# Latent attention's keys, queries and values: per head in plain fp32, or per head pair from split operands through memory

## The chip, the cores and the metric

The program runs on one core of one Trainium2 chip. The metric is the device time of the whole program in microseconds (us), as the median of several runs. Engines are named as in the profile: PE (matmuls), PEld (its weight loads, which overlap PE), DVE, ACT, POOL, and SP, whose queue issues every DMA here.

## The reference

Two layers of a diffusion backbone over 1024 latent tokens and 256 context tokens (T = 1280), all in fp32. Each layer projects the modulated tokens, mixes them in three head groups, projects the result, and runs a gated convolution feed-forward. The change touches one of the three groups, latent attention, with 8 heads of 64 + 32 dimensions:

```
cq = _rms_norm(p[9], mla_q_norm_g)
q = _heads(jnp.einsum('blr,re->ble', cq, mla_w_uq), MLA_HEADS)
qn, qr = q[..., :MLA_D_NOPE], q[..., MLA_D_NOPE:]
ckv = _rms_norm(p[10], mla_kv_norm_g)
kn = _heads(jnp.einsum('blr,re->ble', ckv, mla_w_uk), MLA_HEADS)
v = _heads(jnp.einsum('blr,re->ble', ckv, mla_w_uv), MLA_HEADS)
...
s = (jnp.einsum('bqhd,bkhd->bhqk', qn, kn)
     + jnp.einsum('bqhr,bkr->bhqk', qr, kr)).astype(jnp.float32) * MLA_SCALE
p = jax.nn.softmax(s, axis=-1).astype(v.dtype)
return jnp.einsum('bhqk,bkhe->bqhe', p, v)
```

The rank of `cq` is 256 (two tiles of 128 rows) and that of `ckv` 128 (one tile). Layer 1 (the second) needs no context queries, so its queries begin at token 256.

## The kernel before

**Precision.** Most products are made from split operands: a tensor is held as `hi` (the value rounded to the type float32r, by an ACT cast) plus `lo` (the rest, by a DVE subtraction), which is `split`, L211 to L213. A product is then three float32r matmuls: hi times hi, hi times lo, lo times hi. The large projections (`dense`, L323) and the attention scores (L919) work so. A matmul of plain fp32 operands is one instruction in the program and two in the trace.

**Stages.** A layer goes through the input projection in two halves of 640 tokens (`proj`, a step for each 128 columns), linear attention and retention (`lin`), latent attention (`mla`), the output projection, and the feed-forward. `lin` and `mla` are Python generators: `mla` makes its first two steps at steps 11 and 12 of the second half's `proj` (`MLA_AT`), `lin` starts at step 13, and afterwards `weave` emits 1.1 steps of `lin` for each of `mla`. The Tile framework then schedules the emitted instructions: each engine's order is fixed when the program is built, and an engine runs its list in order. SP's queue is in order too: a DMA that waits for its data holds back all behind it.

**Latent attention.** `S.ckv` and `S.cq` are plain fp32 tiles in the pool `y` (8 buffers of 128 x 1280). For every pair of heads `prod_v` makes the values: 10 plain fp32 matmuls of 128 x 128 (L849) and two ACT copies (L852). For every four heads `prod_qr` makes the rotated part of the queries (L861, and L868 for the rotation). For every head `prod_kq` makes keys (64 rows, L894) and queries (64 rows, two terms, L897) and splits them out of PSUM by ACT (L903) and DVE (L904), each on 64 partitions. The product work of head h + 1 is the `side` generator of head h. Its rotated rows come by small DMAs from one SBUF tile to another (L883).

**A unit** is 128 queries of one head: scores (L919, three PSUM banks, the two halves of six banks in turn), maxima (DVE, L921 and L924), exponentials (ACT, L932), ten transposes (PE, L945), their copies (DVE L947, ACT L949), and the products with the values (L969). `lin_states` turns the linear group's keys in groups of two chunks: a DVE product, PE transposes (L600), an ACT copy (L602), PE products (L608), ACT copies (L615), all through one PSUM bank.

Pools that matter: `t` (6 buffers, shared by all passing results), `hid` (16), `y` (8), `h` (8: keys of two heads, queries of two heads), `wst` (4, raw weights; here 3 of them hold latent attention's weights to the end of the stage).

Of the kernel before, what the change touches and what calls it, by code (L numbers as in the profile page):

```python
# [19 lines left out]
T = 1280  # L20
# [54 lines left out]
class Net:  # L75
# [50 lines left out]
    def ws(self, shape):  # L126
        return self.sb.tile(shape, F32, tag="wst", bufs=4, name=self.nm("ws"))
# [37 lines left out]
    def wplan(self):  # L165
        """The split weights in the order of their use."""
# [81 lines left out]
    def ada(self, l, sets, alloc=None):  # L248
        """Modulation, for both kinds of tokens, of 1024 features at a time: of a section, or of a half of sections 0 and 1."""
# [39 lines left out]
    def modulate(self, l, sec, c0, c1, src, F):  # L289
        """F[k] = src(k) * (1 + scale) + shift; src(k) may be F[k] itself."""  # L290
# [25 lines left out]
    def dense(self, ps, segs, wu, h, ks=range(8)):  # L316
        """ps[:, i, :n] = w.T @ h[:, o:o + n] over 8 K tiles, or the ks of them, for the i-th (o, n) of segs."""
# [8 lines left out]
    def rstd(self, ps, segs, scale, eps, al):  # L326
        """(sum * scale + eps) ** -0.5 in SBUF."""
# [14 lines left out]
    def now(self, g):  # L342
        """The value of a generator that is emitted at once."""
# [14 lines left out]
    def begin(self, h, n):  # L358
        """The first half of K for the first n tiles of the projection: steps for their weights, then for a K tile of one."""
# [11 lines left out]
    def proj(self, l, b, h, S):  # L371
        """A step for every tile of the projection's columns."""
# [24 lines left out]
        def rms(tiles, segs, gcol, kn):  # L397
# [4 lines left out]
            for t in tiles:  # L402
                s = self.tt([128, W])
                nc.scalar.activation(s[:], t[:, c0 + o0:c0 + o0 + W], AF.Square)
# [4 lines left out]
            for i, t in enumerate(tiles):  # L409
                v = t[:, c0 + o0:c0 + o0 + W]  # L410
                nc.vector.scalar_tensor_tensor(v, v, self.vec[l][:, gcol + i:gcol + i + 1], r[:], op0=ALU.mult, op1=ALU.mult)

        def t3():
# [11 lines left out]
            # sums of log gates within chunks, [0] from the right and [1] from the left  # L425
# [59 lines left out]
        def copied(segs, dst):  # L485
            ps = mt(segs)
            for i, (o, n) in enumerate(segs):
                nc.scalar.copy(dst[:, c0 + o:c0 + o + n], ps[:, i, 0:n])

        late = []  # L490
        for m in PORDER:
# [12 lines left out]
            elif m == CKV:  # L504
                copied(full, S.ckv)
                g = None
            elif CQ <= m < CQ + 2:
                copied(qseg, S.cq[m - CQ])
# [23 lines left out]
            if m == CKV:  # L532
                late.append(lambda: rms([S.ckv], full, V_KVG, 1))
            if m == CQ + 1:
                late.append(lambda: rms(S.cq, qseg, V_QG, 2))
# [5 lines left out]
    def lin_tables(self, l, S):  # L541
# [10 lines left out]
        # rows of iota: t + 1, 127 - t, 128 - t, t;  lg: 0..1 by partition (fwd, bwd), 2 + 4 * dir + head  # L552
# [18 lines left out]
    def lin_states(self, l, S):  # L571
        """The chunks' k^T v sums, and from them the state before every chunk, in both directions."""
# [4 lines left out]
        for g in range(5):  # L577
# [4 lines left out]
            for r in range(2):  # L582
# [27 lines left out]
                # the sums lie where the state after their chunk belongs  # L610
# [18 lines left out]
    def lin_chunk_out(self, S, r, c, qv, cs, v, rhs, oS):  # L629
        """o (pair, chunk) = states' part + rhs(h)'s part, into oS."""  # L630
# [44 lines left out]
    def gla_out(self, l, S, g):  # L675
# [11 lines left out]
        def factors(ns):  # L687
            """[0]: q's factor exp(sum from the middle of its block of 2n), [1]: k times its factor."""
# [19 lines left out]
        def expands(i, ns):  # L708
            """q of every head in rows of its own, times its factor."""
# [46 lines left out]
        # products of neighbours and of equal tokens: their sums over a head are columns  # L756
# [69 lines left out]
    def mla(self, l, S):  # L826
        nc, a = self.nc, self.a
        ww = []
        for k, n in (("uqn", 512), ("uqr", 256), ("ukv", 512)):
            t = self.ws([128, 2, n])  # L830
            nc.sync.dma_start(t[:], a[k][l])
            ww.append(t)
        wn, wr, wk = ww
        Kt = [[self.hs([128, T]) for _ in range(2)] for _ in range(2)]
        lo = 0 if l == 0 else CTX
        V, Q, QR, ob = {}, {}, {}, {}
        flip = [0]

        def three(keep=False):
            b = flip[0] ^ 3  # L840
            if not keep:
                flip[0] = b
            return self.ps[:, b:b + 3, :].rearrange("p a b -> p (a b)")

        def prod_v(p):
            V[p] = [self.hid([128, 5, 128]) for _ in range(2)]
            ps = three(keep=True)
            for t_ in range(10):
                nc.tensor.matmul(ps[:, 128 * t_:128 * t_ + 128], S.ckv[:, 128 * t_:128 * t_ + 128], wk[:, 1, 128 * p:128 * p + 128],  # L849
                                 start=True, stop=True)  # L850
            for i in range(2):
                nc.scalar.copy(V[p][i][:].rearrange("p a b -> p (a b)"), ps[:, 640 * i:640 * i + 640])  # L852
            yield

        def prod_qr(x):
            QR[x] = [self.yk(F32R), self.yk(F32R)]
            ps, raw = three(keep=True), QR[x][1]
            chunks = [(o, min(512, T - o), ps[:, o - lo:min(512 + o, T) - lo]) for o in range(lo, T, 512)]
            for o, n, t in chunks:
                for kc in range(2):  # L860
                    nc.tensor.matmul(t, wr[:, kc, 128 * x:128 * x + 128], S.cq[kc][:, o:o + n], start=(kc == 0), stop=(kc == 1))  # L861
                nc.scalar.copy(raw[:, o:o + n].bitcast(F32), t)
            for o, n, t in chunks:
                r = raw[:, o:o + n].bitcast(F32)
# [7 lines left out]
                self.split(QR[x][0][:, o:o + n], raw[:, o:o + n], r)  # L872
                del t2, co, si
            yield

        def prod_kq(h):
            K = Kt[h % 2]
            Q[h] = [self.hs([128, T]) for _ in range(2)]
            rr = slice(32 * (h % 4), 32 * (h % 4) + 32)
            for x in range(2):  # L880
                for o in range(lo, T, 512):
                    c = slice(o, min(o + 512, T))
                    nc.sync.dma_start(Q[h][x][64:96, c].bitcast(F32), QR[h // 4][x][rr, c].bitcast(F32))  # L883
            if h < 2:
                for b in range(2):
                    cs = slice(640 * b, 640 * b + 640)
                    self.split(K[0][64:96, cs], K[1][64:96, cs], S.kr[b][64:96, :])
            if h == 1:
                S.kr.clear()
            yield  # L890
            ps = three(keep=True)
            for o, t, kb in ((CTX, ps[:, 0:512], 1), (CTX + 512, ps[:, 512:1024], 1), (0, ps[:, 1024:1280], 0)):
                n = 512 if kb else CTX
# [574 lines left out]
```

## Time and profile before

| | |
|---|---|
| time, median of 3 runs | 3469.18 us |
| lowest and highest run | 3468.41 and 3472.6 us |
| the profiled execution: first to last instruction | 3473.9 us |
| PE busy | 3383.5 us, 97% |
| DVE busy | 2227.2 us, 64% |
| ACT busy | 1548.3 us, 45% |
| DMA | 354.95 MB, mean 102 GB/s |
| stage of linear and latent attention, layer 0 | about 275 to 810 us |
| the same, layer 1 | about 2127 to 2608 us |

The profiled execution is a run of its own, and its span is the only time that is known of it. A row of the profile that merges instructions gives their start, the time from the first start to the last end, and their count. In a row of windows each engine has its busy time and its number of instructions.

### The profile page before, as it was taken

The numbers are of one execution on the slowest core, as the hardware profiler recorded it, in microseconds if no ns is written. First come the engines' busy times: TensorE is split into PE (matmuls) and PEld (weight loads), VectorE is DVE, ScalarE is ACT, GpSimd is POOL, SyncE is SP. The second block draws the span as 40 slices with busy tenths as digits, with TensorE's granted clock in tenths as the row PEclk, the third lists the DMA queues.
The fourth block names the chain that finished last, engine by engine and source line by source line (L and its number), as shares of the span: only waits on it lengthen the run. The fifth ranks groups of instructions, "written<-read, shape, count | busy, mean of one in ns | idle before, by whom it ended". The sixth has DMA issues, their size and how long they took to land. (4 is left out here: it accounts for less than half of the span.)

```text
span 3473.9 us, 58101 instructions
## 1 busy us (share of the span) xinstructions
PE 3383.5 (97%) x23454; PEld 2919.4 (84%) x23454; DVE 2227.2 (64%) x3787; ACT 1548.3 (45%) x2867; POOL 398.5 (11%) x627
## 2 busy tenths in 40 slices
PE   8999999989999999999999999999999999999998
PEld 6997666768999999899999898766777888888897
DVE  3435878776774444675557734788877765687555
ACT  3334555544453333343334444555563544345433
POOL 0000333331010000000000000333310000001001
PEclk9999999989999999999999999999999999999999
DMA  8654111124223333432223444111124333323331
GB/s 291 203 185 135 29 55 41 40 83 141 74 73 116 122 116 132 147 104 78 75 73 120 161 135 136 36 42 51 38 96 131 96 92 97 97 91 116 98 92 49
DMA packets 174990, 354.95 MB, mean 102 GB/s; under 512 B 15552, under 2 KB 92160, under 8 KB 174720
## 3 DMA queue, kind: packets, MB, share of 16 engines
q1 hardware_dynamic: 174720, 351.23, 31.7%
q8 instruction: 184, 3.01, 0.4%
q14 instruction: 86, 0.70, 0.1%
HBM read 310.01 MB, written 36.44 MB: 100 GB/s over the span
## 5 line engine op out<-in xcount | busy, mean ns | idle before, releaser
L323 PE MATMUL ps<-h,w 128*128 128x320 f32 (+5 forms) x9600 | 1667.4, 334 | 15.1 <-ACT h L212 6.3
L323 PEld LDWEIGHTS ps<-h,w 128*128 128x128 f32 x9600 | 1532.0, 190 | 145.7 <-issue 7.0
L213 DVE TENSOR_TENSOR w<-ws,w 128x1024 fp32r<-128x1024 f32 x360 | 440.1, 1223 | 590.5 <-PE ps L323 294.5
L1180 PE MATMUL ps<-hid,w 128*128 128x256 f32 (+4 forms) x3696 | 576.6, 316 | 1.5 <-ACT hid L212 1.5
L1180 PEld LDWEIGHTS ps<-hid,w 128*128 128x128 f32 x3696 | 538.9, 189 | 36.1 <-issue 7.6
L212 ACT CAST w<-ws 128x1024 fp32r<-128x1024 f32 x360 | 378.8, 1053 | 416.6 <-PE ps L1180 291.2
L919 PE MATMUL ps<-h,h 96*128 96x512 f32 (+1 forms) x1200 | 325.4, 392 | 18.7 <-DVE w L947 14.4
L919 PEld LDWEIGHTS ps<-h,h 96*128 96x128 f32 x1200 | 200.0, 194 | 78.1 <-issue 21.1
L1147 DVE SCALAR_TENSOR_TENSOR t<-u,vec,t 128x642 f32<-128x642 f32 (+3 forms) x176 | 144.6, 821 | 181.9 <-ACT t L1146 181.8
L932 ACT ACTIVATE w<-ps,sm 128x768 f32<-128x768 f32 (+2 forms) x272 | 208.9, 774 | 113.0 <-DVE sm L928 91.2
L1141 ACT COPY u<-ps 128x512 f32<-128x512 f32 (+4 forms) x264 | 118.2, 483 | 310.7 <-PE ps L323 310.7
L1185 DVE SCALAR_TENSOR_TENSOR y<-ps,mod,y 128x320 f32<-128x320 f32 (+5 forms) x376 | 197.0, 557 | 69.0 <-PE ps L1180 68.3
L945 PE MATMUL ps<-ident,w 128*128 128x128 f32 x1312 | 222.3, 287 | 12.1 <-ACT w L932 12.0
L945 PEld LDWEIGHTS ps<-ident,w 128*128 128x128 f32 x1312 | 152.0, 144 | 70.6 <-issue 35.5
L965 POOL TENSOR_SCALAR dg<-ident,sm 128x128 f32<-128x128 f32 x144 | 99.8, 697 | 954.7 <-DVE sm L963 833.4
L1137 POOL MEMSET u<- 128x1 f32 (+1 forms) x264 | 20.9, 102 | 1616.9 <-DVE t L1148 1462.4
L969 PE MATMUL ps<-w,hid 128*64 128x128 f32 x2624 | 196.8, 282 | 3.8 <-DVE y L979 2.0
L969 PEld LDWEIGHTS ps<-w,hid 128*64 128x64 f32 x2624 | 151.8, 139 | 41.2 <-issue 29.1
L921 DVE TENSOR_REDUCE sm<-ps 128x1 f32<-128x1024 f32 x128 | 156.3, 1221 | 43.8 <-PE ps L919 38.8
L949 ACT COPY w<-ps 128x256 f32<-128x256 f32 (+1 forms) x272 | 128.2, 474 | 94.0 <-PE ps L945 92.0
L716 POOL TENSOR_TENSOR hid<-hid,hid 128x512 f32<-128x512 f32 x108 | 146.3, 1371 | 98.5 <-ACT hid L696 69.0
L1146 ACT ACTIVATE t<-u,vec 128x642 f32<-128x642 f32 (+3 forms) x176 | 153.8, 874 | 0.4
(195 smaller groups left out, 3279.4 us busy)
## 6 DMA issues: line engine op xcount, KB each, us to landing
ws<-in_up_dram SPq DMA_DIRECT2D x176, 512.0 KB, 3.6
ws<-in_down_dram SPq DMA_DIRECT2D x88, 512.0 KB, 3.5
ws<-in_ada_dram SPq DMA_DIRECT2D x80, 512.0 KB, 4.8
ws<-in_w_in_dram SPq DMA_DIRECT2D x48, 512.0 KB, 4.3
ws<-in_w_out_dram SPq DMA_DIRECT2D x32, 512.0 KB, 3.7
y<-in_ada_dram SPq DMA_DIRECT2D x16, 512.0 KB, 8.3
ws<-in_w_v_dram SPq DMA_DIRECT2D x16, 512.0 KB, 4.0
hid<-in_xT_dram SPq DMA_DIRECT2D x16, 320.0 KB, 6.1
```

The lines of the kernel that those rows point to most:

```text
L212: self.nc.scalar.copy(hi, src)
L213: self.nc.vector.tensor_tensor(lo, src, hi.bitcast(F32), op=ALU.subtract)
L323: nc.tensor.matmul(ps[:, i, 0:n], w_[:, k, :], h[k][:, part, o:o + n], start=(k == 0 and q == 0), stop=(k == 7 and q == 2))
L716: nc.gpsimd.tensor_tensor(X[n][:], blk(E[n][:, 0, cs[i]]), qx[:], op=ALU.mult)
L919: nc.tensor.matmul(sc[:, o:o + n], q[qa][0:96, qs], K[ka][0:96, o:o + n], start=(x == 0), stop=(x == 2))
L921: nc.vector.tensor_reduce(st[:, 1:2], sc[:, 0:1024], axis=AX.X, op=ALU.max)
L932: nc.scalar.activation(P[:, c0:c1], sc[:, c0:c1], AF.Exp, bias=st[:, 2:3], scale=MSCALE, accum_out=st[:, 3 + j:4 + j])
L945: nc.tensor.transpose(ps[:, t_], P[:, 128 * (t0 + t_):128 * (t0 + t_) + 128], self.ident[:])
L969: nc.tensor.matmul(op[64 * i:64 * i + 64, 0], V[h // 2][t_ // 5][:, t_ % 5, r:r + 64], pts[i][:, t_], start=(t_ == 0), stop=(t_ == nk - 1) ...
L1146: nc.scalar.activation(v[:, 0:n], u[:, 1:1 + n], AF.Identity, scale=cw(j, 1), bias=self.vec[l][:, V_CB + j:V_CB + j + 1])
L1180: nc.tensor.matmul(pb[i][:, 0:n], w[w_][:, x, ms], p.hh[f0 + x][hp][:, o - 1:o - 1 + n], start=(x == 0 and q == 0), stop=(x == gn - 1 and ...
L1185: nc.vector.scalar_tensor_tensor(t, pb[i][:, o:o + n], self.md(l, 5, m, who), t, op0=ALU.mult, op1=ALU.add)
```

## The change

Latent attention's low-rank inputs and its weights are now held split, and its products are made as three float32r matmuls for a pair of heads (128 rows at once) or, for the values, for all heads (512 columns at once). The results go out of PSUM as split pairs into `t` tiles and by DMA into DRAM tiles (`S.kq`, `S.qr`, `S.vm`); each head's keys and queries, and each pair's values, come back by DMA.

- `copied` puts the projected columns into `hid` tiles; `rms` normalises there and splits into `S.ckv` (2 tiles of `y`) and `S.cq` (4 tiles of `y`).
- `first()` makes all keys, all values, the rotated queries of heads 0 to 3 and the queries of pair 0, and loads head 0. `rest()`, the side work of head 0, makes all other queries. Heads 1 to 7 have loads alone as side work (`following`).
- The products use one bank at a time of the three that are free (`bank`).

The core of the diff (lines in which only a comment goes are left out):

```diff
+        def rms(tiles, segs, gcol, kn, dst):
...
+                v, c = t[:, o0:o0 + W], slice(c0 + o0, c0 + o0 + W)
                 nc.vector.scalar_tensor_tensor(v, v, self.vec[l][:, gcol + i:gcol + i + 1], r[:], op0=ALU.mult, op1=ALU.mult)
+                self.split(dst[i][0][:, c], dst[i][1][:, c], v)
...
+        def prod_v():
+
+            t = [self.hid([128, 512], F32R) for _ in range(2)]
+            weight("v", a["ukv"][l][:, 1], [[x[:]] for x in t], 1)
+            for t_ in range(10):
+                p = bank()
+                for x, (wa, ca) in enumerate(order):
+                    nc.tensor.matmul(p, S.ckv[ca][:, 128 * t_:128 * t_ + 128], W["v"][wa][0], start=(x == 0), stop=(x == 2))
+                s = self.tt([128, 512])
+                nc.scalar.copy(s[:], p)
+                nc.sync.dma_start(S.vm[:, t_, :], s[:])
...
+        def product(p, o, n, terms):
+            for x, (w_, c) in enumerate(terms):
+                nc.tensor.matmul(p, w_, c[:, o:o + n], start=(x == 0), stop=(x == len(terms) - 1))
...
+        def to_memory(p, y, o0, terms):
+
+            for o in range(o0, T, 512):
+                n = min(512, T - o)
+                t = bank()[:, 0:n]
+                product(t, o, n, terms)
+                hi, lw = self.tt([128, 512], F32R), self.tt([128, 512], F32R)
+                self.split(hi[:, 0:n], lw[:, 0:n], t)
+                for x, s in enumerate((hi, lw)):
+                    nc.sync.dma_start(S.kq[:, p, y, x, o:o + n], s[:, 0:n].bitcast(F32))
...
-        def prod_kq(h):
-            K = Kt[h % 2]
...
-                nc.tensor.matmul(t[0:64, 0:n], wk[:, 0, 64 * h:64 * h + 64], S.ckv[:, o:o + n], start=True, stop=True, skip_group_check=True)
-                if o >= lo:
-                    for kc in range(2):
-                        nc.tensor.matmul(t[64:128, 0:n], wn[:, kc, 64 * h:64 * h + 64], S.cq[kc][:, o:o + n],
...
+            for x in range(2):
+                nc.sync.dma_start(Kt[h % 2][x][0:64].bitcast(F32), S.kq[rows, h // 2, 0, x])
+                nc.sync.dma_start(Q[h][x][0:64, lo:T].bitcast(F32), S.kq[rows, h // 2, 1, x, lo:T])
+                nc.sync.dma_start(Q[h][x][64:96, lo:T].bitcast(F32), S.qr[rot, h // 4, x, lo:T])
...
+        def first():
+            weights()
+            prod_k(0)
+            yield
+            prod_qr(0)
+            prod_q(0)
+            load(0)
+            yield
+            prod_v()
+            yield
+            for p in (1, 2, 3):
+                prod_k(p)
+            load_v(0)
+            S.ckv.clear()
+            yield
```

How the instructions stand now. PE at the entry of layer 0's latent attention, before: a group of `lin_states` (L600 its transposes, L608 its products, `hid` its keys) has scores (L919) and transposes (L945) between its parts.

```order
L600 MATMUL ps<-ident,hid_2980 128x128 x4
L919 MATMUL ps<-h_2549,h_3032 128x256
L945 MATMUL ps<-ident,w_3094 128x128 x2
L608 MATMUL ps<-hid_2978,hid_2986 32x64 x16
L945 MATMUL ps<-ident,w_3112 128x128 x2
L969 MATMUL ps<-w_3096,hid_2552 64x128
L919 MATMUL ps<-h_2548,h_3032 128x512
```

PE at the same place now (L992 is the scores' new line, L604 and L612 are L600 and L608, L872 is the values' product): five groups follow the first scores, and the values' 30 matmuls follow them.

```order
L992 MATMUL ps<-h_2567,h_2774 128x256
L604 MATMUL ps<-ident,hid_2948 128x128 x4
L612 MATMUL ps<-hid_2946,hid_2956 32x64 x16
L604 MATMUL ps<-ident,hid_3034 128x128 x4
L612 MATMUL ps<-hid_3032,hid_3040 32x64 x16
L604 MATMUL ps<-ident,hid_3068 128x128 x4
L612 MATMUL ps<-hid_3066,hid_3076 32x64 x16
L604 MATMUL ps<-ident,hid_3102 128x128 x4
L612 MATMUL ps<-hid_3100,hid_3108 32x64 x16
L604 MATMUL ps<-ident,hid_3137 128x128 x4
L612 MATMUL ps<-hid_3135,hid_3152 32x64 x12
L872 MATMUL ps<-hid_3154,y_374 128x512
```

No other work of PE stands between the parts of those five groups any more; behind L872's 30 matmuls come the 27 of the keys of pairs 1 to 3. SP's queue at that entry, before: loads for `lin_states` (L584, L586, L580) between the small moves into a head's query tile (L883).

```order
L580 DMA u_2939<-gB_91 128x2x256
L883 DMA h_3032<-y_2620 32x256
L883 DMA h_3033<-y_2621 32x512 x2
L584 DMA hid_2908<-rqk_90 128x256
L586 DMA hid_2910<-v_88 128x2x256
L883 DMA h_3033<-y_2621 32x256
L883 DMA h_3212<-y_2620 32x512 x2
```

SP's queue now, at the end of the keys' products of pairs 1 to 3 (L930 stores a split part of them, L881 loads the values of pair 0, L588 and L590 are L584 and L586).

```order
L930 DMA kq_372<-t_3297 128x512
L930 DMA kq_372<-t_3298 128x512
L930 DMA kq_372<-t_3306 128x512
L930 DMA kq_372<-t_3307 128x512
L930 DMA kq_372<-t_3315 128x256
L930 DMA kq_372<-t_3316 128x256
L881 DMA hid_3321<-vm_373 128x5x128
L881 DMA hid_3322<-vm_373 128x5x128
L588 DMA hid_3325<-rqk_90 128x256
L590 DMA hid_3327<-v_88 128x2x256
```

The load of the first values has moved behind all 10 stores of values and all 18 stores of these keys.

## Rows read from the trace of the kernel before

**Rows 1.** The page's first part: busy time of each engine.

```profile
PE 3383.5 (97%) x23454; PEld 2919.4 (84%) x23454; DVE 2227.2 (64%) x3787; ACT 1548.3 (45%) x2867; POOL 398.5 (11%) x627
```

**Rows 2.** Windows: both attention stages; then clock granted, DMA share, GB/s.

```profile
285.00:345.00 60.00, 55.30 (x542) 38.55 (x541) 39.48 (x82) 32.10 (x93) 3.80 (x5) 0.97 0.48 148
345.00:810.00 465.00, 439.72 (x3683) 320.27 (x3682) 363.15 (x792) 248.86 (x637) 166.37 (x174) 0.97 0.17 52
2140.00:2200.00 60.00, 55.32 (x573) 41.22 (x571) 39.16 (x85) 30.70 (x92) 3.29 (x5) 0.86 0.40 121
2200.00:2550.00 350.00, 337.91 (x2870) 244.71 (x2870) 285.25 (x580) 190.97 (x467) 127.90 (x130) 1.00 0.15 44
2550.00:2608.00 58.00, 57.23 (x539) 46.79 (x538) 44.39 (x102) 39.09 (x93) 8.82 (x12) 1.00 0.32 110
```

**Rows 3.** Product matmuls by line: counts, nanoseconds min/median/max, first and last start, forms.

```profile
L849 PE MATMUL ps<-ws,y x160: 272/275/377, 275.0 to 2493.2; 128*128 128x128 f32 x160
L861 PE MATMUL ps<-y,ws x40: 379/592/697, 282.9 to 2362.9; 128*128 128x512 f32 x32, 128*128 128x256 f32 x8
L894 PE MATMUL ps<-y,ws x96: 378/592/644, 308.6 to 2541.8; 128*64 128x512 f32 x64, 128*64 128x256 f32 x32
L897 PE MATMUL ps<-y,ws x160: 379/592/645, 312.9 to 2542.8; 128*64 128x512 f32 x128, 128*64 128x256 f32 x32
```

**Rows 4.** Chain that ended last: plain fp32 products in unbroken runs (512 columns at L861).

```profile
2126.60 2.23 PE ps L849 x20
...
2134.50 3.43 PE ps L861 x8
```

**Rows 5.** Timeline of PE: float32r matmuls of 256 and of 512 columns, unbroken.

```profile
261.78 13.36 PE L454 MATMUL ps<-w,h 128*128 128x256 f32 x112
...
2845.89 44.48 PE L323 MATMUL ps<-h,w 128*128 128x512 f32 x192
```

**Rows 6.** By line: ACT and DVE work on products, and casts and subtractions of 512.

```profile
L852 ACT COPY hid<-ps x16: 669/698/712, 277.0 to 2493.9; 128x640 f32<-128x640 f32 x16
L862 ACT COPY y<-ps x10: 372/585/586, 284.9 to 2363.6; 128x512 f32<-128x512 f32 x8, 128x256 f32<-128x256 f32 x2
L903 ACT CAST h<-ps x56: 348/1005/1013, 316.6 to 2545.8; 64x1024 fp32r<-64x1024 f32 x32, 64x256 fp32r<-64x256 f32 x24
L904 DVE TENSOR_TENSOR h<-ps,h x56: 402/1216/1226, 317.6 to 2547.7; 64x1024 fp32r<-64x1024 f32 x32, 64x256 fp32r<-64x256 f32 x24
L212 ACT CAST y<-y x10: 406/619/622, 292.2 to 2370.9; 128x512 fp32r<-128x512 f32 x8, 128x256 fp32r<-128x256 f32 x2
L213 DVE TENSOR_TENSOR y<-y,y x10: 424/692/694, 292.8 to 2372.1; 128x512 fp32r<-128x512 f32 x8, 128x256 fp32r<-128x256 f32 x2
```

**Rows 7.** Timeline: one group of lin_states.

```profile
301.45 0.60 PE L600 MATMUL ps<-ident,hid 128*128 128x128 f32 x4
...
302.14 0.59 ACT L602 COPY hid<-ps 128x512 f32<-128x512 f32 x1 [1.87 <-PE ps L600]
...
302.78 0.65 PE L608 MATMUL ps<-hid,hid 128*32 128x64 f32 x32
...
303.50 0.56 ACT L615 COPY y<-ps 128x64 f32<-128x64 f32 x4 [0.24 <-PE ps L608]
```

**Rows 8.** DMA issues: count, size each, median us from issue to landing.

```profile
hid<-v SPq DMA_DIRECT2D x20, 256.0 KB, 4.1
...
m<-hid SPq DMA_DIRECT2D x18, 256.0 KB, 2.1
h<-y SPq DMA_DIRECT2D x64, 64.0 KB, 2.0
```

**Rows 9.** Windows: layer 1's entry, and the stretch with the busiest DMA.

```profile
2160.00:2170.00 10.00, 7.83 (x92) 4.01 (x91) 7.63 (x13) 6.11 (x17) 0.00 (x0) 0.99 0.62 202
2170.00:2180.00 10.00, 8.91 (x56) 6.52 (x54) 6.53 (x13) 2.31 (x8) 0.00 (x0) 0.50 0.39 115
2180.00:2190.00 10.00, 9.58 (x101) 7.89 (x102) 5.89 (x16) 7.00 (x22) 1.26 (x2) 0.66 0.21 66
1960.00:1980.00 20.00, 18.25 (x107) 17.36 (x105) 17.66 (x29) 9.74 (x15) 2.09 (x2) 0.96 0.96 346
```

More of the change, by code (lines that the diff above doesn't have):

```diff
@@ L532, in proj @@
             if m == CKV:
[L533 removed]
+                late.append(lambda: rms(ckv, full, V_KVG, 1, [S.ckv]))
             if m == CQ + 1:
[L535 removed]
+                late.append(lambda: rms(cq, qseg, V_QG, 2, S.cq))
             yield
@@ L845, in prod_v, with weight @@
-        def prod_v(p):
+        lo = 0 if l == 0 else CTX
+        order = ((0, 0), (0, 1), (1, 0))
+        W = {}
+        def weight(key, src, t, parts):
+            for p in range(parts):
+                raw = self.tt([128, 512])
+                nc.sync.dma_start(raw[:], src[:, p] if parts > 1 else src)
+                self.split(t[0][p], t[1][p], raw[:])
+            W[key] = t
+        Kt = [[self.hs([128, T]) for _ in range(2)] for _ in range(2)]
+        V, Q, ob = {}, {}, {}
+        flip, ring = [0], [0]
@@ new lines, in three, with weights @@
+        def three():
+            flip[0] ^= 3
+            return self.ps[:, flip[0]:flip[0] + 3, :].rearrange("p a b -> p (a b)")
+        def weights():
+            t = [self.hid([128, 512], F32R) for _ in range(2)]
+            weight("r", a["uqr"][l].rearrange("p k n -> p (k n)"), [[x[:]] for x in t], 1)
+            t = self.ws([128, 2, 512], F32R)
+            weight("k", a["ukv"][l][:, 0], [[t[:, 0]], [t[:, 1]]], 1)
+            t = [self.ws([128, 2, 512], F32R) for _ in range(2)]
+            weight("n", a["uqn"][l], [[x[:, 0], x[:, 1]] for x in t], 2)
@@ new lines, in bank @@
+        def bank():
+            ring[0] = (ring[0] + 1) % 3
+            return self.ps[:, (flip[0] ^ 3) + ring[0], :]
+        def prod_v():
+            t = [self.hid([128, 512], F32R) for _ in range(2)]
+            weight("v", a["ukv"][l][:, 1], [[x[:]] for x in t], 1)
[6 more added lines that the diff above has]
+                nc.sync.dma_start(S.vm[:, t_, :], s[:])
+            W.pop("v")
@@ L846, in prod_v, with load_v @@
+        def load_v(p):
             V[p] = [self.hid([128, 5, 128]) for _ in range(2)]
[L847 to L850, printed above, removed]
             for i in range(2):
-                nc.scalar.copy(V[p][i][:].rearrange("p a b -> p (a b)"), ps[:, 640 * i:640 * i + 640])
-            yield
+                nc.sync.dma_start(V[p][i][:], S.vm[:, 5 * i:5 * i + 5, 128 * p:128 * p + 128])
@@ L863, in prod_qr @@
-            for o, n, t in chunks:
-                r = raw[:, o:o + n].bitcast(F32)
+            terms = [(W["r"][wa][0][:, 256 * kc + 128 * x:256 * kc + 128 * x + 128], S.cq[kc][ca]) for kc in range(2) for wa, ca in order]
+            for o in range(lo, T, 512):
+                n = min(512, T - o)
+                t = bank()[:, 0:n]
+                product(t, o, n, terms)
+                raw = self.hid([128, 512], F32R)
+                r = raw[:, 0:n].bitcast(F32)
+                nc.scalar.copy(r, t)
@@ L905, in prod_kq, with rest, following @@
+        def rest():
+            load(1)
+            S.kr.clear()
+            prod_q(1)
+            yield
+            prod_q(2)
+            yield
+            prod_qr(1)
+            yield
+            prod_q(3)
+            S.cq.clear()
+            yield
+        def following(h):
+            load(h)
+            if h % 2 == 0:
+                load_v(h // 2)
             yield
@@ L917, in scores @@
                 n = min(512, nk - o)
-                for x, (qa, ka) in enumerate(order):
+                for x, (ka, qa) in enumerate(order):
                     nc.tensor.matmul(sc[:, o:o + n], q[qa][0:96, qs], K[ka][0:96, o:o + n], start=(x == 0), stop=(x == 2))
@@ L983, in values @@
                 nc.sync.dma_start(S.m[:, 4 + h // 2, c0:c1], o[:, c0:c1])
-        def chain(*gs):
-            for g in gs:
-                yield from g
-        for _ in chain(prod_v(0), prod_qr(0), prod_kq(0)):
+        for _ in first():
             yield
@@ L1285 @@
         nc.sync.dma_start(S.gw[64:96], a["gw"][l])
-        S.cq = [net.yk(), net.yk()]
-        S.ckv = net.yk()
+        S.qr = net.dp.tile([128, 2, 2, T], F32, name=f"qr{l}")
+        S.kq = net.dp.tile([128, 4, 2, 2, T], F32, name=f"kq{l}")
+        S.vm = net.dp.tile([128, 10, 512], F32, name=f"vm{l}")
+        S.ckv = [net.yk(F32R) for _ in range(2)]
+        S.cq = [[net.yk(F32R) for _ in range(2)] for _ in range(2)]
         F = []
```

89 lines of the change are left out of this document (30 added, 59 removed).

## The prediction, on record before the run

> **What bounds the kernel now.** I read the page's first part for the whole span, then windows over the two stages that the change touches, then the chain of waits. PE is busy for 97% of the span and no other engine for more than 64% [rows 1]. In the windows of linear and latent attention the reader is to see the same: of 993 us PE is busy for 945, DVE for 771, and even the last stretch, where latent attention runs alone, is PE's (57.2 of 58.0 us) [rows 2]. So a microsecond taken from PE there is worth nearly one, unless its list then waits. The slack is unequal, though: DVE is at 78 and 82% in the long stretches of both layers, and PE already stands idle for 25 of 465 and 12 of 350 us there [rows 2].
>
> **What is removed from PE.** The products' records by line are 160, 40, 96 and 160 [rows 3]; a plain fp32 matmul is two records. One record costs 2.23 / 20 = 0.112 us at 128 columns and 3.43 / 8 = 0.429 at 512 [rows 4]; at 256 I take half, 0.214. Values (L849): 160 x 0.112 = 17.8 us. Rotated queries (L861): 32 x 0.429 + 8 x 0.214 = 15.4. Keys (L894): 64 x 0.429 + 32 x 0.214 = 34.3. Queries (L897): 128 x 0.429 + 32 x 0.214 = 61.8. Together 129.3 us over both layers. The rotation (L868) stays as it is.
>
> **What is added to PE.** Three terms per product, but for two heads at once. Keys are 24 matmuls of 512 and 12 of 256 columns a layer, queries 48 and 24 in layer 0 and 48 and none in layer 1, rotated queries 24 and 12, then 24 and none, values 30 of 512 a layer: 252 of 512 and 60 of 256 columns. A float32r matmul costs 44.48 / 192 = 0.232 us at 512 and 13.36 / 112 = 0.119 at 256 [rows 5]: 58.4 + 7.2 = 65.6 us. **PE saves 129.3 - 65.6 = 64 us**, about 34 in layer 0 and 30 in layer 1.
>
> **ACT and DVE.** Casts and subtractions now work on 128 partitions. DVE loses L904, 32 x 1.22 + 24 x 0.40 = 48.7 us, and gets 32 x 0.69 + 12 x 0.42 = 27.2 for keys and queries, 10 x 0.69 for the split weights and, scaled from 512 to 640 columns, at most 12 x 0.87 for the splits in `rms` [rows 6]: 5 us less. ACT loses L903, 40.5, and L852, 11.2; it gets 24.7 + 6.2 + 9 in the same way and 20 x 0.585 for the values' copies [rows 6]: about nothing. The splits in `rms` lie beside the projection's matmuls; if that cover were gone, they would cost 12 x 0.77 = 9 us. Neither engine pays for PE's saving, and neither gains as much as PE does.
>
> **What is added as waits: the entry of the stage.** All 64 us come out of heads 0 to 7, but the new waits stand in one place, between the last projections and the first full units of head 0, once per layer.
>
> (a) Five groups of `lin_states` now stand on PE with nothing between their parts. A group takes from 301.45 to 303.50 + 0.56 = 304.06, 2.61 us, of which PE works 1.25 [rows 7]; they share one PSUM bank, so the next cannot start sooner. 5 x 1.36 = 6.8 us a layer, 13.6 in all. Before, scores stood between. Bounds: 0, if their loads and steps are ready early and the bank's reader is quicker, and 20, if SP's queue, in which these loads stand behind head 0's, brings them later.
>
> (b) Keys of pairs 1 to 3: nine parts in a row, each needing two of the six `t` buffers until its two stores have landed. A buffer is held for a cast 0.62, a subtraction 0.69 and a landing of 2.1 us for 256 KB, with queueing some 4 us [rows 6, 8]; three parts are in flight, so nine take 12 us against 6 x 3 x 0.232 + 3 x 3 x 0.119 = 5.2 of matmuls. 6.8 a layer, 13.6 in all. Bounds: 0 and 30 (DMA below). The values' ten parts need one buffer each, and ACT's 10 x 0.585 is below PE's 30 x 0.232 = 7.0 [rows 5, 6]: 0.
>
> (c) The first scores wait for head 0's stores and loads, and the first products with values for the load of the values behind the keys' 18 stores. A store of 256 KB lands in 2.1 us and a load in 4.1 [rows 8]: 6.2. Head 0's is covered in the main by two parts of pair 1's queries and projections (I take 2 us open in layer 0, 1 in layer 1), the values' by about 4 us of scores and queries (1.5 open in each): 6 us. Bounds: 0 and 25.
>
> [...]
>
> (d) PE's clock. After a stretch with PE at 7.8 of 10 us, the granted clock was 0.50 and then 0.66 for 10 us each [rows 9], so the level of 1.2 GHz instead of 2.4 for about 17 us, which costs some 8 us of matmuls. Layer 1's entry pays this already, layer 0's mostly not (0.97) [rows 2]. I take 6 us more for layer 0. Bounds: 0 and 20.
>
> **Sum.** (a) to (d) are 13.6 + 13.6 + 6 + 6 = 39 us. The heads' later boundaries lose their product bursts and get a higher share of DVE; I let these cancel. 64 - 39 = 25 us. The profiled execution of 3473.9 us would become 3449; the median before is 4.7 us below that span, so the median after is 3444 us.
>
> **Rivals.**
>
> The entry is hidden. If the loads come early and the `t` buffers turn round in 2 us, the waits are 15 us or less, and the time falls by 49 us or more: 3405 to 3420. For it: DMA moves only 52 GB/s in the long stretch, and the entry had 121 to 148 [rows 2]. Against it: the order of PE's list, in which nothing can fill the gaps.
>
> DMA saturates at the entry, and the kernel is slower. Keys, values, the first queries and rotated queries, and two heads' loads are 5.2 + 2.6 + 2.6 + 1.3 + 3.2 = 15 MB a layer on top of the 148 GB/s that flow there [rows 2]. The fastest row of 20 us moved 346 GB/s at a share of 0.96 [rows 9]: 15 MB at the 200 GB/s left over take 75 us, of which PE's own work at the entry covers some 55 at best. If they are exposed for more than 64 / 2 = 32 us a layer, the change loses; at 40 a layer the time is 3469 + 16 = 3485. For it: (a), (b) and (c) all stand behind the same queue. Against it: most of those bytes are needed only by later heads, and only the `t` buffers make PE wait for their stores.
>
> DVE takes over. In the long stretches DVE would be busy for some 360 of 431 us (84%) in layer 0 and 282 of 320 (88%) in layer 1 [rows 2]. Where its in-order list sets the pace, a stretch shortens only by what DVE itself loses there, 48.7 - 27.2 - 6.9 = 15 us in place of 64. If that holds for half of them, the gain is (64 + 15) / 2 = 40, and the entry's 39 takes it all: 3468, and between 3462 and 3476 with its bounds. For it: PE's idle time in the long stretches. Against it: the scores need no more of DVE than before, and its list loses its pieces of 1.22 us, behind which maxima waited.
>
> **How the numbers follow.** The forecast, waits of 20 to 55 us, has 0.55: 3425 to 3462. The hidden entry has 0.20, DVE's case and others that end near zero 0.13, saturation 0.12. The range from 3412 to 3470 leaves out part of the hidden case's best (0.10) and most of the slower one (0.10). Runs of this kernel lie within 4 us, so 0.2%, 7 us, is about what can be told from no change: faster is 0.55 + 0.20 + a little of DVE's case = 0.77, slower 0.12 less what ends near zero, 0.10, same 0.13.
>
> **What would show it.** The new product lines should have about 310 records of 0.23 and 0.12 us, and PE's busy time in both stages should fall by 60 to 65 us. PE's idle time between the last projection and the first full units should rise by 10 to 20 us a layer, under `lin_states`' transposes and the keys' products, with waits on ACT, DVE and `t` stores. From head 1 on, PE's idle time should be as before. I would be wrong if the keys' parts come at PE's own pace (then the gain is larger), or if the long stretches lose PE's saving to waits on DVE (then smaller).

## The result, and the profile after

The changed kernel takes 3497.4 us (median of 4 runs, 3494.2 to 3503.4), the kernel before 3468.8 (4 runs, 3466.0 to 3472.6): a ratio of 1.0084, 95% interval 1.0070 to 1.0099. It is 29 us slower; 25 us faster had been forecast. The profiled execution has a span of 3492.3 us, 18.4 more than the one of before. The account below goes by these two profiles and so explains 18.4 of the 29 us: the one of before is a little slower than its 4 timed runs, the one of the changed kernel is the fastest of its 4.

The page of the changed kernel, first part [rows 1]:

```profile
PE 3363.4 (96%) x23310; PEld 2932.7 (84%) x23310; DVE 2225.3 (64%) x3797; ACT 1549.2 (44%) x2881; POOL 399.4 (11%) x627
```

PE's busy time fell by 3383.5 - 3363.4 = 20.1 us only. Its idle time, span less busy, rose from 90.4 to 128.9, by 38.5. Both together are the 18.4 us. So the waits came out near the 33 us that (a), (b) and (c) made, while of the saving of 64 us less than a third is left.

Windows of the changed kernel over the attention stages, in the columns of [rows 2]. The later starts and ends allow for what it is late:

```profile
285.00:345.00 60.00, 41.88 (x371) 34.12 (x370) 27.66 (x50) 22.31 (x67) 0.00 (x0) 0.75 0.84 240
345.00:822.00 477.00, 444.52 (x3783) 334.24 (x3784) 364.51 (x814) 255.63 (x669) 171.44 (x179) 0.95 0.34 101
2152.00:2212.00 60.00, 40.55 (x371) 31.16 (x369) 24.68 (x47) 27.44 (x76) 0.00 (x0) 0.72 0.80 235
2212.00:2567.00 355.00, 335.41 (x2948) 253.48 (x2948) 291.60 (x613) 190.18 (x489) 129.47 (x134) 0.98 0.34 98
2567.00:2625.00 58.00, 57.23 (x542) 46.83 (x540) 43.58 (x101) 39.90 (x94) 8.84 (x12) 1.00 0.27 91
```

In the entries PE stands idle for 18.1 and 19.5 of 60 us, where it was 4.7 and 4.7; its clock is 0.75 and 0.72, where it was 0.97 and 0.86; the DMA share is about twice what it was. The long stretches have some 15 us more idle time than before. Where it lies shows when the stages are cut at each layer's first exponential. Up to there, of the kernel before and then of the changed one:

```profile
275.00:325.00 50.00, 46.66 (x403) 36.28 (x401) 27.23 (x51) 23.45 (x65) 0.00 (x0) 0.97 0.53 164
2127.00:2179.85 52.85, 48.74 (x429) 37.27 (x427) 29.43 (x51) 24.34 (x70) 0.00 (x0) 0.90 0.55 167
```

```profile
275.00:366.44 91.44, 69.78 (x541) 56.80 (x539) 39.40 (x73) 39.03 (x102) 0.00 (x0) 0.81 0.79 245
2139.00:2219.78 80.78, 57.44 (x458) 44.43 (x456) 35.08 (x62) 33.17 (x89) 0.00 (x0) 0.79 0.83 254
```

Here PE's idle time rose from 3.3 to 21.7 us in layer 0 and from 4.1 to 23.3 in layer 1, 37.5 of the 38.5 us. Head 0 adds 1.8 and 0.9 us; in heads 1 to 7 of both layers together it is 32.9 us, where it was 30.3. This is where the prediction put the waits, and near its 10 to 20 us a layer. Once their products are done the heads are faster: the exponentials of head 0's middle unit start 59.5 us later than before (415.9 against 356.4), those of layer 0's last unit 12.4 us later (831.2 against 818.8).

The same kernel, timeline of PE in layer 0's entry; in brackets the idle time ahead and what ended it:

```profile
321.52 0.66 PE L992 MATMUL ps<-h,h 96*128 96x256 f32 x2 [2.26 <-DMA h<-qr]
323.21 1.12 PE L604 MATMUL ps<-ident,hid 128*128 128x128 f32 x4 [1.03 <-DVE hid L597]
325.00 1.08 PE L612 MATMUL ps<-hid,hid 128*32 128x64 f32 x32 [0.68 <-ACT hid L606]
327.82 1.09 PE L604 MATMUL ps<-ident,hid 128*128 128x128 f32 x4 [1.74 <-DVE hid L599]
329.58 1.08 PE L612 MATMUL ps<-hid,hid 128*32 128x64 f32 x32 [0.68 <-ACT hid L606]
332.47 1.11 PE L604 MATMUL ps<-ident,hid 128*128 128x128 f32 x4 [1.81 <-DVE hid L597]
...
345.38 0.87 PE L612 MATMUL ps<-hid,hid 128*32 128x64 f32 x24 [0.73 <-ACT hid L606]
346.17 8.48 PE L872 MATMUL ps<-hid,y 128*128 128x512 f32 x30
```

Five groups of lin_states stand alone, as (a) said, but one takes 4.6 us and not 2.6 [rows 7], with its PE parts 1.1 us each and not 0.6. Two windows of 10 us inside show why these are long, and how busy DMA is:

```profile
320.00:330.00 10.00, 4.36 (x58) 3.08 (x62) 3.52 (x7) 2.67 (x9) 0.00 (x0) 0.58 1.07 328
330.00:340.00 10.00, 4.93 (x99) 3.53 (x88) 2.43 (x6) 2.70 (x10) 0.00 (x0) 0.50 1.07 220
```

PE is busy for 4.4 and 4.9 of 10 us, and the granted clock is 0.58 and then 0.50, the level of 1.2 GHz. By line, with busy time, mean ns of a record and idle time ahead, the groups' two kinds of matmuls:

```profile
L612 PE MATMUL ps<-hid,hid 128*32 128x64 f32 x640 | 18.7, 275 | 9.5 <-ACT hid L606 9.5
L604 PE MATMUL ps<-ident,hid 128*128 128x128 f32 x80 | 17.9, 366 | 20.7 <-DVE hid L597 11.6 <-DVE hid L599 9.1
```

PE waits 9.5 + 20.7 = 30.2 us ahead of them in the program. For the same two lines of the kernel before it was 4.6 + 2.6 = 7.2:

```profile
L608 PE MATMUL ps<-hid,hid 128*32 128x64 f32 x640 | 14.8, 241 | 4.6 <-ACT hid L602 3.6 <-DMA hid<-v 0.9
L600 PE MATMUL ps<-ident,hid 128*128 128x128 f32 x80 | 14.0, 304 | 2.6 <-DVE hid L593 2.1 <-DVE hid L595 0.4
```

### The profile page after: what moved, and what is told of

The parts are those of the page before. It is cut to its first block, busy times and chain, and to the rows that moved or that the text cites. A ratio compares the mean times of both kernels' runs of the same rounds, so it can differ in the third digit from the quotient of the medians.

```text
span 3492.3 us, 58230 instructions
## 1 busy us (share of the span) xinstructions
PE 3363.4 (96%) x23310; PEld 2932.7 (84%) x23310; DVE 2225.3 (64%) x3797; ACT 1549.2 (44%) x2881; POOL 399.4 (11%) x627
## 4 chain that ended last, share of the span: by engine, by line
PE 84%; DVE 8%; DMA 3%; ACT 2%; issue 2%; SPq 0%; POOL 0%; DVEq 0%; POOLq 0%; ACTq 0%
PE ps L323 45%; PE ps L1242 16%; PE ps L992 5%; PE ps L1042 3%; PE ps L1018 3%; PE ps L457 3%; PE ps L263 1%; PE ps L647 1%; DVE sm L994 1%; DVE hid L707 1%; PE ps L651 1%; PE ps L885 1%; DMA ws<-in_ada_dram 1%; DVE hid L697 1%; ACT w L1005 1%
## 5 line engine op out<-in xcount | busy, mean ns | idle before, releaser
L992 PE MATMUL ps<-h,h 96*128 96x512 f32 (+1 forms) x1200 | 330.3, 395 | 31.6 <-DVE w L1020 11.3
L992 PEld LDWEIGHTS ps<-h,h 96*128 96x128 f32 x1200 | 198.7, 194 | 89.3 <-issue 21.5
```

The source lines that it names most:

```text
L992: nc.tensor.matmul(sc[:, o:o + n], q[qa][0:96, qs], K[ka][0:96, o:o + n], start=(x == 0), stop=(x == 2))
```

## The experiments

Each ran beside the kernel before; ratios are to it. Several set only one line of the changed kernel:

```diff
-LIN_FROM, LIN_STEPS, MLA_AT = 13, 10, (11, 12)
+LIN_FROM, LIN_STEPS, MLA_AT = 13, 4, (11, 12)            # e1; e11 in the kernel before
+LIN_FROM, LIN_STEPS, MLA_AT = 13, 10, (11, 12, 13, 14)   # e2
+LIN_FROM, LIN_STEPS, MLA_AT = 13, 4, (11, 12, 13, 14)    # e8
+LIN_FROM, LIN_STEPS, MLA_AT = 13, 10, (10, 11, 12, 13)   # e9
+LIN_FROM, LIN_STEPS, MLA_AT = 13, 10, (9, 10, 12, 14)    # e10
```

**Did keys cost PE what was reckoned? (e5)** In the timeline of PE of the kernel before, a head's keys (L894) and queries (L897):

```profile
396.94 0.64 PE L894 MATMUL ps<-y,ws 128*64 128x512 f32 x1
396.94 0.64 PE L897 MATMUL ps<-y,ws 128*64 128x512 f32 x1
397.42 0.59 PE L894 MATMUL ps<-y,ws 128*64 128x512 f32 x1
397.42 0.59 PE L897 MATMUL ps<-y,ws 128*64 128x512 f32 x1
397.85 0.59 PE L894 MATMUL ps<-y,ws 128*64 128x512 f32 x1
397.85 0.59 PE L897 MATMUL ps<-y,ws 128*64 128x512 f32 x1
```

Two records of 0.6 us start together, and the next two only 0.43 to 0.48 us later: with 64 output rows each, keys into partitions 0 to 63 and queries into 64 to 127, they run side by side. 62 of the 96 records for keys start within 0.06 us of one for queries, 60 of them within 0.014 us. The Trainium skill says so on its page "TensorE: Matmul & The Clock Gate", under "Why this matters for your kernels": matmuls with few output rows, placed at different column groups, run at the same time. The trace agrees, with starts 0.005 to 0.014 us apart.

```diff
 for o, t, kb in parts:
     n = 512 if kb else CTX
     nc.tensor.matmul(t[0:64, 0:n], wk[:, 0, 64 * h:64 * h + 64], S.ckv[:, o:o + n], start=True, stop=True, skip_group_check=True)
+for o, t, kb in parts:
+    n = 512 if kb else CTX
     if o >= lo:
```

> The kernel before, with a head's matmuls for keys all written ahead of those for its queries, where they alternated. In the trace of before 62 of the 96 records for keys start within 0.06 us of one for queries, on the other half of the columns, and keys cost PE 17 us and not the 34 that were reckoned. Theory D (keys ran beside queries, so that making them for head pairs saves less): with the pairs apart some 40 of these records take 0.43 us of their own, 12 to 18 us more, 3481 to 3487 against 3469. If the records' starts say nothing of what PE does, no change: 3469 within 7 us.

3484.3 us, 1.0041 (1.0029 to 1.0054): 14 us more than before, in the range of D. In its profile 34 records still run beside one, and by the reckoning below (a record counts until the next one starts) keys and queries take 83.4 us of PE in place of 71.4. So parting some of the pairs already cost 12 to 14 us: running side by side was worth at least this much, and the change had less to save.

**Do the groups that stand alone cost it? (e1, e2, e11)**

> The changed kernel with LIN_STEPS 4 instead of 10, so that fewer groups of lin_states are emitted ahead of the values' products: in PE's list one group in layer 0 and two in layer 1 stand alone before the values, where five and five stood. Theory A (the groups stand alone on PE, and each waits for the one before through DVE's in-order list): four and three groups of some 4.7 us go away there and come back among scores with PE's own 1.25 us each, so 33 - 9 = 24 us less, 3473 us, and the stretch with PE half idle falls from some 27 to some 8 us in layer 0. Theory B (the stores and loads of the new products fill the DMA engines at the entry): the same bytes move in the same place, so 3497 within 7 us.

> The changed kernel with all four first steps of latent attention placed in the projection's steps 11 to 14 instead of two in 11 and 12, so that values and the keys of pairs 1 to 3 are emitted before most of lin_states. Theory A (groups alone on PE): products and projections now stand between the groups, so some 20 to 30 us less, 3467 to 3477. Theory B (DMA full at the entry): the stores come earlier and compete with the loads of linear attention and of weights, so no gain or a loss, 3495 or more.

3487.7 us, 1.0045 (1.0032 to 1.0057), and 3481.3 us, 1.0030 (1.0021 to 1.0040). Both win back, 10 and 16 us, less than A had. The control:

> A control: the kernel before with LIN_STEPS 4 instead of 10. In the trace of before the groups already stand among projections and scores, so moving them should give nothing: 3469 within 7 us. If it gains 10 us as the changed kernel did, the gain there was not from groups that stood alone.

3493.6 us, 1.0072 (1.0059 to 1.0085). A miss: LIN_STEPS 4 by itself costs the kernel before 24 us. If it costs the changed kernel as much, not standing alone gained more than 10 us in e1; no run shows whether it does. With LIN_STEPS 4 in both, the changed kernel is some 6 us faster than the kernel before (3487.7 against 3493.6, ratios 1.0045 and 1.0072); with 10 in both it is 29 slower.

**Is it the lower clock? (e4)**

```diff
+if 2 <= 2 * g + r <= 6:   # behind the transposes
+    nc.tensor.matmul(self.pb("av"), self.ident[:], kk[:].rearrange("p d c t -> p (d c t)"), start=True, stop=True)
...
+if 2 <= 2 * g + r <= 6:   # behind the products
+    for _ in range(2):
+        nc.tensor.matmul(self.pb("av"), self.ident[:], kn[:].rearrange("p d c t -> p (d c t)"), start=True, stop=True)
```

> The changed kernel with three idle-filling matmuls of 512 columns per group (float32, results never read) in the five groups of lin_states that stand alone, so that PE works on and its clock need not fall. Theory C (the lower clock is what costs at the entry): the granted clock of the stretch rises from 0.54 to 0.9 or more, the group's two PE parts shrink from 2.2 to 1.25 us, values and keys run at 0.23 us a matmul: 5 to 8 us less a layer, 3481 to 3487 in all. Theory A without the clock (waits between engines set the pace): no change, 3497 within 7 us, or slower by the fillers' own time of up to 1.3 us a group, 3510.

3497.7 us, 1.0074 (1.0060 to 1.0088). Windows of the two stretches with groups, of e4 and then of the changed kernel:

```profile
320.00:350.00 30.00, 27.05 (x217) 15.25 (x218) 7.63 (x16) 11.40 (x33) 0.00 (x0) 0.89 0.89 224
2180.00:2200.00 20.00, 19.97 (x173) 11.36 (x173) 5.65 (x13) 9.29 (x25) 0.00 (x0) 1.00 0.62 169
```

```profile
320.00:350.00 30.00, 15.12 (x185) 11.02 (x186) 8.60 (x18) 8.90 (x29) 0.00 (x0) 0.54 0.77 199
2180.00:2200.00 20.00, 12.01 (x147) 8.74 (x146) 4.80 (x11) 6.87 (x21) 0.00 (x0) 0.53 0.52 117
```

The clock stands at 0.89 and 1.00, where the changed kernel had 0.54 and 0.53, and layer 0's values take 7.24 us and not 8.48; the time is the same. At full clock the fillers took 3.0 us of PE in a group, where at most 1.3 had been reckoned, so this does not price the clock; but a faster PE did not shorten the entry.

**Is it transfers? (e3, e6, e7, e17)**

```diff
 nc.sync.dma_start(S.kq[:, p, y, x, o:o + n], s[:, 0:n].bitcast(F32))
+nc.sync.dma_start(S.kq2[:, p, y, x, o:o + n], s[:, 0:n].bitcast(F32))   # e3, and so for S.vm
```

> The changed kernel with every store of keys, queries and values made twice, the second into memory that nobody reads: 12 MB a layer more, some 9 MB of it at the entry. Theory B (DMA full at the entry is what costs): 9 MB at the 300 GB/s seen there are 30 us more a layer, so 3540 to 3560 us. Theory A (groups alone on PE): the stretch with the groups stays as it is, only the keys' parts wait longer for their buffers, 0 to 10 us a layer, so 3497 to 3517.

3551.0 us, 1.0229 (1.0215 to 1.0243): 54 us more than the changed kernel, as B said. So bytes that are added to DMA there are paid nearly in full; what the change's own bytes cost, this does not show.

```diff
-nc.sync.dma_start(S.kq[:, p, y, x, o:o + n], ...)
+if y or not p:                                      # e6; loads read S.kq[rows, 0, 0, x]
+    nc.sync.dma_start(S.kq[:, p, y, x, o:o + n], ...)
+nc.scalar.dma_start(S.kq[:, p, y, x, o:o + n], ...) # e7, and so for S.vm and S.qr
```

> The changed kernel without the stores of the keys of pairs 1 to 3; their heads load the keys of pair 0 instead. Left out: three quarters of the keys that heads work with. 18 stores, 3.9 MB a layer, are gone from the entry, while PE's list stands as it was and all loads remain. Theory B (DMA full at the entry): at 300 GB/s 13 us a layer come back, 3470 to 3478. Theory A (groups of lin_states alone on PE): these stores come behind the groups, so only the waits for t buffers between the keys' parts go, 3 to 5 us a layer, 3487 to 3491.

3490.6 us, 1.0058 (1.0044 to 1.0072): 7 us less, as A said. The stores behind the groups are not the bulk. (Heads 2 to 7 of this run work with the keys of pair 0; it leaves work out and only prices it.)

> The changed kernel with the stores of keys, queries, rotated queries and values issued by ACT instead of SP, so that SP's queue holds no issue that waits for a split and the loads of linear attention and of head 0 are issued as soon as their buffers are free. If SP's order holds back the loads at the entry: 5 to 12 us less a layer, 3473 to 3487. Theory B (bandwidth): the same bytes, 3497 within 7 us. If ACT's list now stands still at issues: slower than 3504.

3529.7 us, 1.0168 (1.0155 to 1.0182): 32 us slower. Either SP's order is not what holds the loads, or moving the stores costs more than it gains: PE waited 31 us for lin_states' multiplications (L597, L599), where it was 21. The Trainium skill's page "DMA: Bandwidth & Descriptors" ("Issuing engines are not separate DMA queues") says that transfers issued by any engine share the same DMA engines; no gain in this run speaks against it.

What sets a group's pace was tried last. In DVE's list of the changed kernel a state update (L626) waits for the group before, and the next group's multiplication (L599) stands behind it:

```profile
326.39 0.67 DVE L626 SCALAR_TENSOR_TENSOR y<-y,cs 128x64 f32<-128x64 f32 x2 [3.24 <-ACT y L619]
326.99 0.69 DVE L599 TENSOR_TENSOR hid<-hid,hid 128x512 f32<-128x512 f32 x1
```

e17 moves the updates to POOL:

```diff
-nc.vector.scalar_tensor_tensor(st[r][:, d, nx, :], st[r][:, d, c, :], dec, st[r][:, d, nx, :], ...)
+nc.gpsimd.tensor_scalar(x[:, 0:64], st[r][:, d, c, :], dec, None, op0=ALU.mult)
+nc.gpsimd.tensor_tensor(st[r][:, d, nx, :], st[r][:, d, nx, :], x[:, 0:64], op=ALU.add)
```

> The changed kernel with the state updates of lin_states (multiply and add of 64 columns, 64 a layer) on POOL as two instructions instead of one on DVE. PE's list at the entry stays as it was, five groups alone; in DVE's list the next groups' subtraction and multiplications now follow one another. If DVE's list sets the groups' pace: from 4.7 to some 3.0 us a group, 7 to 9 us a layer, 3479 to 3484. If the shared PSUM bank, the loads or the clock set it: 3497 within 7 us.

3514.5 us, 1.0132 (1.0110 to 1.0153). DVE in layer 0's entry of e17:

```profile
322.67 0.69 DVE L597 TENSOR_TENSOR hid<-hid,hid 128x512 f32<-128x512 f32 x1 [3.14 <-DMA hid<-gqk]
326.46 0.69 DVE L599 TENSOR_TENSOR hid<-hid,hid 128x512 f32<-128x512 f32 x1 [3.09 <-DMA hid<-rqk]
...
335.05 0.69 DVE L599 TENSOR_TENSOR hid<-hid,hid 128x512 f32<-128x512 f32 x1 [3.15 <-DMA hid<-rqk]
...
341.47 0.69 DVE L597 TENSOR_TENSOR hid<-hid,hid 128x512 f32<-128x512 f32 x1 [5.12 <-DMA hid<-gqk]
```

The updates are gone from the list, and the groups come hardly faster: the first five start within 18.8 us (323.42 to 342.21), where it was 20.3 (323.21 to 343.53). Now they wait for their loads of 128 KB, which the update's wait had covered: in the changed kernel four of these loads had landed only 0.7 to 3.0 us before the multiplications that read them. (The 17 us more are in head 0, where PE stands idle for 21.3 and 11.3 us in place of 9.2 and 3.0; the updates that are late on POOL are the likely cause.) The same loads, DMA issues over the whole program of the kernel before, and then of the changed kernel:

```profile
u<-gB SPq DMA_DIRECT2D x19, 256.0 KB, 3.2
hid<-gqk SPq DMA_DIRECT2D x10, 128.0 KB, 3.8
hid<-rqk SPq DMA_DIRECT2D x10, 128.0 KB, 3.3
```

```profile
u<-gB SPq DMA_DIRECT2D x19, 256.0 KB, 5.7
hid<-gqk SPq DMA_DIRECT2D x10, 128.0 KB, 5.8
hid<-rqk SPq DMA_DIRECT2D x10, 128.0 KB, 5.0
```

Unchanged loads take 1.7 to 2.5 us longer. In layer 0's entry the linear group's loads issued between 324 and 333 us took 6.9 to 9.2 us (2.3 to 4.8 in the kernel before, at 301 to 320 us). What is in flight around them is loads and not the new stores: from 311 to 334 us SP issues the twelve loads of heads 0 and 1, and no value and no key of pairs 1 to 3 is stored before 349 us.

**A version that wins? (e8, e9, e10, e12, e13, e15, e16, e18)**

> The changed kernel with latent attention's four first steps in the projection's steps 10 to 13: in PE's list values, keys and head 0's products now lie among projection matmuls and among the groups of lin_states, and scores follow the projection at once. If the waits of the entry come from work that stands alone on PE, its idle time falls from 112 us to some 80, near that of before (73), and with the products' 28 to 40 us less the time is 3445 to 3465, below before. If transfers at the entry set the end of it (stores doubled cost 54 us), the products wait for t buffers in their new place too: 3475 to 3490.

3477.9 us, 1.0025 (1.0016 to 1.0034), in the second range: the best of the changed forms, 20 us faster than the change as made, still some 8 us behind the kernel before. PE's idle time fell only to 124.5 us: ahead of the two layers' first exponentials it is 15 us less than in the changed kernel, in head 0 of the two layers 13 us more. So the waits in the main moved.

> The changed kernel with the four first steps in the projection's steps 9, 10, 12 and 14: head 0's round trip through memory lies under three projection steps, and the keys of pairs 1 to 3 come behind the projection, spread among groups of lin_states. If the round trip and its loads are what the entry waits for, this one is the faster of the two: 3445 to 3460. If the groups and the keys' parts behind the projection are, it lies between e2 and e9: 3465 to 3481.

3483.3 us, 1.0043 (1.0031 to 1.0055): slower than e9 and, with 2 us more, about as e2, so outside both ranges. It gives no sign that the round trip of head 0 is the main wait.

> The changed kernel with both moves together, the four first steps in the projection's steps 11 to 14 and LIN_STEPS 4. If what costs is that lin_states' groups stand without other work on PE, both moves spread them further: 3468 to 3478, below the 3481 of the first move alone. If DMA at the entry has become what costs there, the second move adds nothing: 3481 within 7 us.

3506.8 us, 1.0103 (1.0089 to 1.0117): a miss for both readings; each move alone had gained.

e12 and e13 make the rotated queries of heads 4 to 7 and the queries of pair 3 beside head 1:

```diff
-            prod_qr(1)              # in rest(), beside head 0
-            prod_q(3)
+            if h == 2:              # in following(h), beside head 1
+                prod_qr(1)
+                prod_q(3)
```

> The changed kernel with the rotated queries of heads 4 to 7 and the queries of pair 3 made beside head 1 instead of head 0; the entry stays as it was. If head 0's burst of products is a second place of waits (scores behind the rotation's PSUM banks: 6 us in layer 0), 5 to 8 us less a layer, 3481 to 3487. If the added waits all lie at the entry: 3497 within 7 us.

> Both moves: the four first steps in the projection's steps 10 to 13 (e9: 3478) and half of head 0's burst in head 1. If the two places of waits are separate, their gains add up: 3462 to 3470, at or below the kernel before. If what waits in head 0 is late only because the entry is, nothing is added to e9: 3474 to 3482.

3499.2 us, 1.0075 (1.0061 to 1.0089), and 3492.6 us, 1.0058 (1.0045 to 1.0070). The first gives nothing, the second loses 15 of the 20 us that e9 had won: in layer 0 head 0 took 15 us less than in e9, and head 1 24 us more. (The same move with e2's order, 3495.3 us, did likewise.)

e15 and e16 take the rotation's tables and the low halves from the larger pool `hid` instead of `t`:

> The changed kernel with first steps in the projection's steps 10 to 13 (as e9: 3478) and with the rotation's tables and the low halves of keys and queries in the hid pool. If the six t buffers hold the products' parts: 4 to 8 us less a layer than e9, 3462 to 3470. If transfers or the engines' lists do: 3478 within 7 us.

> The same buffers with the first steps where the changed kernel has them. In PE's list head 0's products now come earlier among the projections, and seven groups of lin_states in layer 0 stand alone ahead of the values instead of five. If the buffers are what costs: 3481 to 3489. If groups that stand alone are: two more of them at 4.7 us, less the 1.25 us that PE works in them wherever they stand, so 7 us slower in layer 0, 3500 to 3508.

3487.9 us, 1.0051 (1.0038 to 1.0063), and 3518.6 us, 1.0136 (1.0120 to 1.0151). More buffers did not help, and e16 is slower than either of its ranges. In e16 seven groups stand alone in layer 0, and PE waits 9.28 us for the first of them:

```profile
324.26 1.11 PE L604 MATMUL ps<-ident,hid 128*128 128x128 f32 x4 [9.28 <-DVE hid L597]
```

> The same with the four first steps in the projection's steps 10 to 13 (e9: 3478). If DVE's list held the groups there as well: 3466 to 3473. If not: 3478 within 7 us.

3508.2 us, 1.0109 (1.0089 to 1.0129): the updates on POOL cost here as well. No version beat the kernel before.

## Why the prediction was wrong

**The step that failed: what is removed from PE.** 129.3 us were taken off, each record of [rows 3] at its unbroken distance. That priced 34.3 us for keys that ran beside queries. Counted from each record's start to the next start, at most its own length, the four lines took 18.8 (values), 15.6 (rotated queries), 16.8 (keys) and 54.6 (queries), 105.8 us in all: 23.5 less than was taken off. Keys and queries together were 71.4 and not 96.1, since they ran side by side; e5, which parted some of the pairs, bears this out. Values and rotated queries were priced rightly. The trace had the sign of it: records of L894 with `128*64`, and the order with L894 and L897 in turn. The busy time by line does not show it, since two records that run at once count twice.

**What is added to PE** was right as far as unbroken runs go: 312 records, at full clock mostly 0.233 us apart at 512 columns. So PE saves 105.8 - 65.6 = 40 us by this price, not 64. The same count over the whole changed kernel gives 77.4 us in place of 65.6.

**(d), the clock, was too small.** 77.4 - 65.6 = 11.8 us on the products, and PE's other work took 3286.0 us in place of 3277.7, 8.3 more: 20 us, where 6 were taken. Not all of it is the clock. Of the products' 11.8 some 4 are 20 records that ran wholly or partly at the lower level, 0.44 us apart; the rest ran at full clock with short waits inside a record's length, which this count takes for work. In all, PE was busy for 97.2 us of the time at the lower level, 61.7 before; half of the 35.5 more, 18 us, is the most that the clock can have added to PE's busy time. It fell where PE stood idle, as (d) said; but layer 1, which was taken to pay already, fell from 0.86 to 0.72 as well.

**(a) was too small, (b) too large, their sum near.** Idle time ahead of the groups' matmuls went from 7.2 to 30.2 us: 23 more, beyond the bound of 20, for 13.6. The group of [rows 7] was read where its loads lay ready. The sentence behind the bound, that the loads come late, is part of what happened: they are slow to land once they are issued, and no run shows that SP's order is the reason (e7). In the changed kernel itself the wait that ends last is DVE's list, with the loads close behind (e17). The parts of keys and queries (L885) wait 5.0 us, 4.0 of it for the splits that free their PSUM banks, and not 13.6; but scores now wait 6.9 us for the rotation and 5.1 for the splits of products whose PSUM banks they need, which no term had. (c): 4.3 us, for 6.

**The sum again:** -105.8 + 65.6 + 20.1 + 38.5 = +18.4 us, the difference of the spans. Against the forecast of 24.5 us less (129.3 - 65.6 - 39.2) that is 42.9 us: 23.5 from the work removed, 14.1 from the slower PE records that stood under (d), 5.3 from the waits. With 64 us saved, the waits and the clock as they came would have left a gain of some 5 us by the profiles.

**The rivals.** Saturation was the nearest, with the other sign and 3485 us. Its mechanism is shown in part: the DMA share is 1.07 in the groups' stretch, loads take longer to land, and added bytes are paid (e3). But taking 18 stores a layer away gave back only 7 us (e6), and part of the 29 us a layer of idle time and slower records comes from the groups' order and from the clock. So that this is near the 32 to 40 us of its price is in part luck; the kernel became slower because the saving was 40 us and not 64. That it was given 0.12 rested on "most of those bytes are needed only by later heads": true, but unchanged loads stood in the same engines. DVE did not take over: from head 1 on PE stands idle for 32.9 us, where it was 30.3, and the heads of layer 0 won back 47 of 59.5 us. The entry was not hidden.

**What stays open.** Why e8, e13 and e15 lost what their parts had won. Each edit there changed the lists of all engines, and no run held them fixed. (In e15 PE's idle time is 3 us less than in e9 and its busy time 11 us more.) How much the clock costs is bounded by 18 us and not measured, since e4's fillers cost PE time. And no run moved the loads of head 1, which stand among the groups' own loads, to a later place; so how much of the groups' waits they cause is not shown.

## What to carry to other kernels

Before you count a half-width matmul as waste, look whether another half-width one starts at the same moment; count PE's work from start to start, not by the busy time of a line (short waits then count as work). Where a change sends intermediates through memory, price the loads of others that are in flight at that time, not only its own. And groups of short dependent work that were hidden between other matmuls can come to stand on the critical path once these leave.

## What the runs showed of the hardware

Two fp32 matmuls of 64 output rows and 512 columns ran at once, with starts 0.005 to 0.014 us apart, each as long as alone (0.59 us), and the next pair began 0.43 to 0.48 us later. Stores that were issued from ACT in place of SP cost 32 us (e7). The DMA share was 1.07 while 220 GB/s were moved (330 to 340 us, loads alone: into 32 and 64 partitions, and of 128 and 256 KB), and 0.96 at 346 GB/s [rows 9]. A load of 320 KB into 64 partitions took 5.2 us in the median, one into 128 partitions 3.6.
